# A two-layer hybrid trunk on one core: the convolution's layer norm, q's projection and the gates in another order

## The chip, the core and the metric

The kernel runs on one core of a Trainium2 chip. The metric is the device time of one launch in microseconds (us); lower is better. The core has five engines that each run their own queue of instructions in order: PE (matrix multiply, with PEld for its weight loads), DVE (vector), ACT (scalar functions and copies), POOL (a second vector engine) and SP, whose queue here starts nearly all the transfers (DMA). An engine that waits for a semaphore holds up all that is queued behind on the same engine.

## What is computed

Two layers over 512 latent tokens and 256 context tokens of width 1024. In each layer a normalised and modulated input feeds three branches, which are gated, added and projected; a gated feed-forward part (FFN) with a short convolution follows. The second layer computes the queries, gates and FFN for the 512 latents only. Cut to what matters:

```
h = modulate(rms_norm(x, g1), sh1, sc1)          # sh, sc, g from silu(c) @ w_mod + b_mod  ("mod")
z_glu, z_qa, z_kva, z_kr, z_gq, z_gk, z_gv, z_gate = split(h @ w_in)
# branch 1: convolution of 31 taps along the tokens, 512 channels
y  = a * sigmoid(g)                               # a, g = split(z_glu)
br_conv = silu(layer_norm(depthwise_conv(y) + b)) @ w_conv_out
# branch 2: MLA, 8 heads;  q from z_qa, k and v from z_kva and z_kr
q_m = rope(rms_norm(rms_norm(z_qa) @ w_q_b));  k_m = rope(rms_norm([k_nope, z_kr]))
# branch 3: GQA, 8 heads on 2 kv heads
q_g = rope(rms_norm(z_gq));  k_g = rope(rms_norm(z_gk))
merged = gate0 * br_conv + gate1 * (softmax(q_m k_m) v_m @ w_mla_o) + gate2 * (softmax(q_g k_g) v_g @ w_gqa_o)
x = x + g1 * merged @ w_out                       # gate = sigmoid(z_gate + b_gate)
x = x + g2 * conv_ffn(modulate(rms_norm(x, g2n), sh2, sc2))
```

## The kernel before

**Products.** A float32 product is made of three matmuls on halves: each operand is split into a rounded part (hi) and the rest (lo), and hi·hi, lo·hi and hi·lo are added in PSUM (`gemm`, L220 in the rows). For a weight block ACT makes hi by a copy (L138) and DVE makes lo by a subtraction (L144).

**The feeder.** Weight blocks of 128x1024 (512 KB) come in by DMA from SP's queue (L191) in the order in which the steps need them. There are 4 raw buffers and 4 pairs of split buffers. A block that is split leaves its raw buffer as soon as hi and lo are made. The blocks of a "mod" step (the adaLN weights, two blocks for each step) are not split: PE multiplies with them as they are (L383), and their two raw buffers come free only when that has run. A next load is asked for when a step has ended.

**Steps and background work.** The program is a list of steps. Before a step's function runs, `pump(budget)` takes closures from a queue `bgq`, whose items carry a cost, until the budget is used up; an item `None` ends the pumping at once. So the order in which the instructions of DVE, ACT and PE stand is fixed when the program is built: a budget decides how many background items stand between two steps. The background work of a layer is, in this order: the taps of the depthwise convolution (one DVE instruction each, L147, name acc), q's norm and rotation (`q_post`), that of GQA's q and k (`g_post`), the layer norm (LN) of the convolution (`ln_start`), and then k's norm (`k_post`), pushed when the attention begins.

**The steps of a layer.** The convolution's input (glu), three blocks of q's latent and two of kv's (`latent`, name z), 12 gate blocks (`gate`, name gt), then the token projections (`tok`: kkv in 3 steps, gq in 4, name tk), q's projection `qproj` (name qp) from three w_qb blocks, 12 more gates, `kvproj`, the attention, the merge of the branches, the out-projection and the FFN. While there are mods left, `bg_step` puts one mod step behind a gate (the first 22 in layer 0) or behind a pair of FFN up blocks j (18 in layer 0's FFN); in layer 1 none are left.

**The layer norm.** `ln_start` pushes: a (sum of the four channel blocks, three DVE instructions, name la), b (two or one matmuls of that sum with ones, name mu), c (deviation and squares), d (column sums by PE, name cs, and rstd on DVE), e (broadcast by PE, name bc, to the tile lrb), and for each channel block g: multiply by rstd on DVE (acc), sigmoid on ACT (L816, name lsg), multiply on DVE, split for the output projection. `ln_check`, called by each gate, starts it at the first gate at which `bgq` is empty. That is gate 22 in layer 0, so that d, e and g are pumped out by the slots of the attention, and gate 20 in layer 1.

**The attention.** 8 groups of two heads; a group has 14 slots in layer 0 and 12 in layer 1. A slot puts out the scores of one key block (L1126, name st), its exponential on ACT (L1133, name pe), the product with v (L1148, name ox), the row maxima of the next heads (matmul L974 on PE, reduction L976 on DVE, name mx, their transposition L995, name mt). In the first three groups each slot also pumps 0.3 of background work; what is left is put out before group 3. `norm1` of a group (L1165, name dx) stands at slot 4 of the next one, so dx marks where a group ends.

Of the kernel before, what the change touches and what calls it, by code (L numbers as in the profile page):

```python
# [96 lines left out]
def trunk_kernel(ctx: ExitStack, tc: tile.TileContext, x_t, ctx_t, cc, vec, grow, ident, rope,  # L97
# [361 lines left out]
    def layer(l):  # L459
# [7 lines left out]
        bud, gbud = (3.3, 4.2) if last else (5.0, 6.5)  # L467
# [145 lines left out]
        for i in range(2):  # L613
            latent(i, "kva", aseg, V_GKVA, 11 + i)

# [73 lines left out]
        def qproj(b):  # L689
# [14 lines left out]
            st.pop("qa")  # L704
            q_post()

        def q_post():
# [33 lines left out]
            g_post()  # L741

        def g_post():
            for (c0, nh, g0, ts_) in ((512, 2, G_GK, 6), (0, 8, G_GQ, nq)):
# [29 lines left out]
                bgq.extend((0.38 * nh, c(t)) for t in range(ts_))  # L774

        def ln_start(_):
# [30 lines left out]
            def g(j):  # L807
                def fn():
                    a_, sg = acc[j], [half("lsg") for _ in qseg]
                    b_ = a_  # L810
                    hi, lo = big("ch", F32R), big("cl", F32R)
                    for s, t in zip(qseg, sg):
                        c0, n, _ = s
                        stt(b_[:, c0:c0 + n], a_[:, cseg(s)], vcol(V_LG + j), z["rb"][:, c0:c0 + n],
                            ALU.mult, ALU.mult)
                        act(out=t[:, 0:n], in_=b_[:, c0:c0 + n], func=AF.Sigmoid, bias=vcol(V_LB + j))  # L816
                        stt(b_[:, c0:c0 + n], b_[:, c0:c0 + n], vcol(V_LB + j), t[:, 0:n], ALU.add, ALU.mult)
                    cpA(hi[:, :nT], b_[:, :nT])
                    tt(P, lo[:, :nT], b_[:, :nT], f(hi[:, :nT]), ALU.subtract)
                    z["o", j] = hi, lo  # L820
# [15 lines left out]
            for j in range(4):  # L836
                if j > 1:
                    bgq.append((0, spill(j - 2)))
                bgq.append((2.0, g(j)))
            bgq.extend([None, (0, spill(2)), None, (0, spill(3))])  # L840
# [6 lines left out]
        def ln_check():  # L847
            if not (bgq or st.get("ln")):
                st["ln"] = True
                ln_start(None)  # L850

        def gate(i):
            br, m = i % 3, i // 3

            def fn(b):
                gate_spill()
                pz = [(psum("gt"), s) for s in qseg]
# [5 lines left out]
                ln_check()  # L863
            add([W(w_gate[l, br * KD + m], 1024)], fn, gbud)
        for i in range(24):
            if i == 12:
                tok(lambda bi, n: w_kkv[l, :, bi * 864:bi * 864 + n], 3, 3, 288, 6, kkv_evac,
                    tb=(4.0, 4.0, 1.0))
                tok(lambda bi, n: w_gq[l, bi], 4, 2, 512, nq, gq_evac, lat_rstd,
                    (2.5, 0.3, 2.5, 1.5) if last else (4.0, 0.5, 4.5, 2.5))  # L870
                add([W(w_qb[l, k], 768) for k in range(3)], qproj, 4.0 if last else 6.0)
            gate(i)
            if i < 22:
                bg_step()

        def attn_pre(_):
            st.pop("H"), st.pop("ln")
# [763 lines left out]
```

## Time and profile before

| | |
|---|---|
| median of 3 runs | 2532.14 us (2530.42 to 2533.91) |
| the profiled execution, its time | 2531.37 us |
| its span, first to last instruction | 2529.6 us |
| PE busy | 2403.5 us (95% of the span) |
| DVE busy | 1464.1 us (58%) |
| ACT busy | 917.8 us (36%) |
| POOL busy | 431.6 us (17%) |
| mean granted clock of PE | 0.971 |

A busy share is an average over stages. Where the share of PE falls, the rows show who it waits for. A line of the timeline gives start, duration, engine, line of the code, and in brackets the idle time ahead of the instruction with what ended it. The granted clock is 1.00 at 2.4 GHz and 0.5 at 1.2 GHz.

### The profile page before, as it was taken

The page shows a single profiled execution, that of the slowest core. Times are in us where ns is not written, and L with a number is a line of the kernel's source. Part 1 is how long each engine was busy: PE and PEld are TensorE (multiplying, and loading weights), DVE is VectorE, ACT ScalarE, POOL GpSimd, SP SyncE. Part 2 cuts the span into 40 slices and gives each one's busy share as a digit, 9 for nine tenths or more (in the row PEclk, how much of TensorE's full clock was granted, in tenths as well). Part 3 has the DMA queues.
Part 4 walks back from the last instruction along what each step waited for, and adds up shares of the span by engine and source line. Part 5 has one row for each costly group of instructions (what it writes and reads, how often), then busy time and mean ns, then how long its engine had stood idle before and what let it go on. Part 6 is the DMA issues. An engine that isn't in the chain of part 4 may idle for free.

```text
span 2529.6 us, 32127 instructions
## 1 busy us (share of the span) xinstructions
PE 2403.5 (95%) x12434; PEld 1885.4 (75%) x12434; DVE 1464.1 (58%) x2522; ACT 917.8 (36%) x1517; POOL 431.6 (17%) x327
## 2 busy tenths in 40 slices
PE   6999999969999999999999999999769999999999
PEld 4887887634568878888888877888534578888887
DVE  5688466666524455444344457887676455655454
ACT  4322232566632234223132333324465523434332
POOL 1000000145544121001000011000046631201000
PEclk9999999979999999999999999999879999999999
DMA  6236336311044413323222233343311154232332
GB/s 254 77 113 210 123 106 206 95 57 58 26 167 142 147 37 100 101 91 118 92 101 92 82 104 102 102 121 103 91 51 39 60 183 139 80 111 78 100 102 72
DMA packets 108740, 267.56 MB, mean 106 GB/s; under 512 B 19574, under 2 KB 28412, under 8 KB 108588
## 3 DMA queue, kind: packets, MB, share of 16 engines
q1 hardware_dynamic: 108588, 265.52, 32.3%
q8 instruction: 98, 1.61, 0.3%
q14 instruction: 54, 0.44, 0.1%
HBM read 231.24 MB, written 31.60 MB: 104 GB/s over the span
## 4 chain that ended last, share of the span: by engine, by line
PE 67%; DVE 8%; ACT 3%; issue 2%; DMA 0%; POOL 0%; SPq 0%; ACTq 0%; POOLq 0%; DVEq 0%
PE up L220 22%; PE pz L220 16%; PE bx L220 7%; PE gt L220 4%; PE st L1126 4%; PE ox L1148 3%; PE tk L634 2%; DVE mx L976 2%; PE mx L974 1%; PE z L220 1%; PE tp L964 1%; PE mod L383 1%; DVE rst L144 1%; PE dx L1165 1%; PE st L1131 1%
## 5 line engine op out<-in xcount | busy, mean ns | idle before, releaser
L144 DVE TENSOR_TENSOR lo<-raw,hi 128x1024 fp32r<-128x1024 f32 (+3 forms) x282 | 345.7, 1232 | 457.7 <-ACT hi L138 451.4
L138 ACT ACTIVATE hi<-raw 128x1024 fp32r<-128x1024 f32 (+4 forms) x298 | 283.5, 963 | 467.9 <-PE pz L220 172.2
L220 PE MATMUL up<-hl,hi 128*128 128x512 f32 (+1 forms) x1088 | 330.8, 352 | 6.5 <-DVE hl L147 5.8
L220 PE MATMUL up<-hh,hi 128*128 128x512 f32 (+1 forms) x1088 | 332.4, 353 | 2.6 <-DVE fc L147 2.6
L220 PE MATMUL up<-hh,lo 128*128 128x512 f32 (+1 forms) x1088 | 330.0, 351 | 0.8 <-DVE lo L144 0.8
L147 DVE SCALAR_TENSOR_TENSOR fc<-up,vct,fc 128x511 f32<-128x511 f32 (+1 forms) x264 | 162.1, 655 | 186.3 <-ACT fc L1460 184.4
L220 PEld LDWEIGHTS up<-hh,hi 128*128 128x128 f32 x1088 | 182.8, 188 | 44.1 <-ACT fc L1460 11.7
L147 DVE SCALAR_TENSOR_TENSOR acc<-y,vct,acc 128x768 f32<-128x768 f32 (+29 forms) x240 | 211.6, 884 | 6.7
L220 PEld LDWEIGHTS up<-hl,hi 128*128 128x128 f32 x1088 | 182.8, 188 | 36.9 <-DVE hl L147 6.6
L220 PEld LDWEIGHTS up<-hh,lo 128*128 128x128 f32 x1088 | 183.0, 188 | 31.0 <-DVE lo L144 1.2
L144 POOL TENSOR_TENSOR gl<-fc,gh 128x768 fp32r<-128x768 f32 (+1 forms) x44 | 69.5, 1579 | 787.0 <-ACT gh L138 767.2
L976 DVE TENSOR_REDUCE mx<-mx 128x1 f32<-128x512 f32 (+1 forms) x288 | 140.4, 533 | 71.3 <-PE mx L974 70.4
L144 POOL TENSOR_TENSOR es<-es,pe 128x512 f32<-128x512 f32 x128 | 164.4, 1292 | 94.7 <-ACT pe L1133 91.5
L220 PE MATMUL gt<-hh,hi 128*128 128x512 f32 x576 | 177.1, 361 | 0.0
L220 PE MATMUL gt<-hh,lo 128*128 128x512 f32 x576 | 174.1, 356 | 1.5 <-DVE lo L144 1.5
L220 PE MATMUL gt<-hl,hi 128*128 128x512 f32 x576 | 174.0, 356 | 0.0
L144 POOL TENSOR_TENSOR es<-pe,pe 128x512 f32<-128x512 f32 x32 | 40.9, 1287 | 770.1 <-DMA raw<-in_w_br_dram 732.6
L220 PE MATMUL pz<-gh,hi 128*128 128x512 f32 (+1 forms) x528 | 163.6, 358 | 0.0
L220 PE MATMUL pz<-gh,lo 128*128 128x512 f32 (+1 forms) x528 | 163.2, 357 | 0.0
L220 PE MATMUL pz<-gl,hi 128*128 128x512 f32 (+1 forms) x528 | 162.7, 356 | 0.0
L1460 ACT ACTIVATE fc<-up,vct 128x512 f32<-128x512 f32 (+1 forms) x132 | 88.3, 703 | 200.6 <-PE up L220 200.6
L1133 ACT ACTIVATE pe<-st 128x512 f32<-128x512 f32 x208 | 122.7, 597 | 87.6 <-PE st L1126 72.0
(282 smaller groups left out, 4362.4 us busy)
## 6 DMA issues: line engine op xcount, KB each, us to landing
raw<-in_w_up_dram SPq DMA_DIRECT2D x88, 512.0 KB
raw<-in_w_mod_dram SPq DMA_DIRECT2D x80, 512.0 KB
raw<-in_w_gate_dram SPq DMA_DIRECT2D x48, 512.0 KB
raw<-in_w_a_dram SPq DMA_DIRECT2D x26, 512.0 KB
gd<-go SPq DMA_DIRECT2D x48, 256.0 KB
gx<-gd SPq DMA_DIRECT2D x48, 256.0 KB
raw<-in_w_dn_dram SPq DMA_DIRECT2D x32, 384.0 KB
raw<-in_w_dn_dram SPq DMA_DIRECT2D x32, 320.0 KB
```

Of the source, the lines that this page charges most:

```text
L138: act(out=o, in_=i, func=AF.Copy, scale=scale)
L144: e.tensor_tensor(out=o, in0=a, in1=b, op=op)
L147: V.scalar_tensor_tensor(out=o, in0=a, scalar=s, in1=b, op0=op0, op1=op1)
L220: mm(p[:, 0:cn], lhsT=w, rhs=a[:, c0:c0 + cn], start=(k == 0 and j == 0), stop=(k == n - 1 and j == 2))
L383: mm(p[32 * j:32 * j + 32, :], lhsT=cs[:, 2 * kt:2 * kt + 32], rhs=b[j // 2][:, (j % 2) * 512:(j % 2 + 1) * 512], start=(kt == 0), stop=(k ...
L634: mm(p[:, 0:ncols], lhsT=a, rhs=ww, start=(k == 0 and q == 0), stop=(k == KD - 1 and q == 2))
L964: nc.tensor.transpose(p[0:rows, i * 128:(i + 1) * 128], src(t0 + i), idn[:])
L976: V.tensor_reduce(out=self.m2[:, o:o + 1], in_=p[:, 0:n], axis=AX.X, op=ALU.max)
L1126: mm(p[:], lhsT=a, rhs=b, start=(k == 0), stop=(k == len(ops) - 1))
L1133: act(out=e[:], in_=p[:], func=AF.Exp, scale=hd.scale)
L1148: mm(self.o[g][64 * j:64 * j + 64, :], lhsT=self.heads[h].v(t), rhs=self.e.pop((h, i))[:], start=(t == 0), stop=(t == 5), tile_position=(0 ...
L1460: act(out=acc[:, c], in_=p[:, 0:s[1]], func=AF.Identity, scale=vcol(o + 1), bias=vcol(V_FB + j + i * KF))
```

## The change

`qproj` and its three weight blocks stand right behind the latents, in front of the gates. `qproj` starts the layer norm itself: the items of LN and of `q_post` are interleaved, and each `None` of LN (a pause before a step that needs a result of another engine) is replaced by about 3.0 of cost of `q_post` items. The items g of LN are split in two (g up to the sigmoid, g2 behind it). `g_post` is queued by a step without blocks behind the gq projection, and its last item sets a mark that `attn_pre` pumps for, so the attention begins with none of this work left. 16 gates, each with a mod in layer 0, stand ahead of the token projections instead of 12, and no mod stands behind the other 8. The six mods that layer 0's gates lose are taken up by its FFN: four of the up pairs (j = 4, 8, 12, 16) are followed by two mods instead of one, and two pairs that had none get one. Some budgets change; `lat_rstd` moves from the second gq step to gate 1.

```
-        bud, gbud = (3.3, 4.2) if last else (5.0, 6.5)
+        bud, gbud = (3.3, 4.4) if last else (5.0, 6.5)
...
             latent(i, "kva", aseg, V_GKVA, 11 + i)
+        add([W(w_qb[l, k], 768) for k in range(3)], lambda b: qproj(b), 4.0 if last else 6.0)
...
             st.pop("qa")
+            k = len(bgq)
             q_post()
+            q = [bgq.pop() for _ in range(len(bgq) - k)]
+            ln_start(None)
+            ln = [bgq.pop() for _ in range(len(bgq) - k)]
+            while ln:
+                x, n = ln.pop(), 3.0
+                while q and x is None and n > 0:
+                    n -= q[-1][0]
+                    bgq.append(q.pop())
+                if x is not None or n == 3.0:
+                    bgq.append(x)
+            bgq.extend(reversed(q))
...
             bgq.extend((2.8, c(t)) for t in range(nq))
-            g_post()
...
                 bgq.extend((0.38 * nh, c(t)) for t in range(ts_))
+            bgq.append((0, lambda: st.update(gd=l)))
...
+                    a_, z["sg", j] = acc[j], [half("lsg") for _ in qseg]
+                    for s, t in zip(qseg, z["sg", j]):
+                        c0, n, _ = s
+                        stt(a_[:, c0:c0 + n], a_[:, cseg(s)], vcol(V_LG + j), z["rb"][:, c0:c0 + n],
+                            ALU.mult, ALU.mult)
+                        act(out=t[:, 0:n], in_=a_[:, c0:c0 + n], func=AF.Sigmoid, bias=vcol(V_LB + j))
+                return fn
+
+            def g2(j):
+                def fn():
+                    a_ = acc[j]
                     hi, lo = big("ch", F32R), big("cl", F32R)
...
+                    for (c0, n, _), t in zip(qseg, z.pop(("sg", j))):
+                        stt(a_[:, c0:c0 + n], a_[:, c0:c0 + n], vcol(V_LB + j), t[:, 0:n], ALU.add, ALU.mult)
+                    cpA(hi[:, :nT], a_[:, :nT])
+                    tt(P, lo[:, :nT], a_[:, :nT], f(hi[:, :nT]), ALU.subtract)
...
-            for j in range(4):
+            for j in range(5):
+                if j < 4:
+                    bgq.append((1.1, g(j)))
+                if j > 0:
+                    bgq.append((1.1, g2(j - 1)))
                 if j > 1:
                     bgq.append((0, spill(j - 2)))
-                bgq.append((2.0, g(j)))
-            bgq.extend([None, (0, spill(2)), None, (0, spill(3))])
+            bgq.extend([None, (0, spill(3))])
...
-        def ln_check():
-            if not (bgq or st.get("ln")):
-                st["ln"] = True
-                ln_start(None)
-
...
                 gate_spill()
+                if i == 1:
+                    lat_rstd()
...
         for i in range(24):
-            if i == 12:
+            if i == 16:
...
-                tok(lambda bi, n: w_gq[l, bi], 4, 2, 512, nq, gq_evac, lat_rstd,
-                    (2.5, 0.3, 2.5, 1.5) if last else (4.0, 0.5, 4.5, 2.5))
-                add([W(w_qb[l, k], 768) for k in range(3)], qproj, 4.0 if last else 6.0)
+                tok(lambda bi, n: w_gq[l, bi], 4, 2, 512, nq, gq_evac, None,
+                    (2.5, 2.5, 2.5, 1.5) if last else (4.5, 4.5, 4.5, 2.5))
+                add([], lambda b: g_post())
             gate(i)
-            if i < 22:
+            if i < 16:
                 bg_step()
...
             gate_spill()
+            while st.get("gd") != l:
+                pump(1e9)
...
-                bg_step()
+                bg_step(2 if j in (4, 8, 12, 16) else 1)
```

Three places of the order. First ACT's queue in layer 0 where the attention begins, before; pe are the exponentials, lsg the sigmoids of LN, ch its split, and a table load stands between the two functions.

```order
L1133 ACTIVATE pe_4498<-st_4495 128x512
L138 ACTIVATE lrb_4515<-bc_4516 128x512
L138 ACTIVATE lrb_4515<-bc_4522 128x256
L816 ACT_TABLE_LOAD
L816 ACTIVATE lsg_4526<-acc_787,vct 128x512
L816 ACTIVATE lsg_4527<-acc_787,vct 128x256
L138 ACTIVATE ch_4528<-acc_787 128x768
L1133 ACT_TABLE_LOAD
L1133 ACTIVATE pe_4541<-st_4538 128x512
L816 ACT_TABLE_LOAD
L816 ACTIVATE lsg_4562<-acc_856,vct 128x512
```

And after, the place where the same sigmoids stand now, behind gate 15 in the first token projection (mrow is the copy of a mod's result, hi that of a weight block):

```order
L138 ACTIVATE lrb_3063<-bc_3064 128x512
L138 ACTIVATE lrb_3063<-bc_3070 128x256
L827 ACTIVATE lsg_3074<-acc_787,vct 128x512
L827 ACTIVATE lsg_3075<-acc_787,vct 128x256
L827 ACTIVATE lsg_3080<-acc_856,vct 128x512
L827 ACTIVATE lsg_3081<-acc_856,vct 128x256
L138 ACTIVATE ch_3086<-acc_787 128x768
L827 ACTIVATE lsg_3092<-acc_981,vct 128x512
L827 ACTIVATE lsg_3093<-acc_981,vct 128x256
L138 ACTIVATE hi_3160<-raw_2981 128x1024
```

The sigmoids of LN now stand among copies, with no exponential near them and no table load between, and in the whole program 16 table loads are gone from ACT.

Second, DVE's queue in layer 1 around a of LN, before; gt is GQA's q under `g_post`, lo are weight blocks.

```order
L144 TENSOR_TENSOR gt_14141<-gt_14141,rt_14967 128x512
L144 TENSOR_TENSOR lo_15003<-raw_14749,hi_15002 128x1024
L144 TENSOR_TENSOR la_15008<-acc_13072,acc_13240 128x512
L144 TENSOR_TENSOR lb_15009<-acc_13078,acc_13162 128x512
L144 TENSOR_TENSOR la_15008<-la_15008,lb_15009 128x512
```

And after:

```order
L147 SCALAR_TENSOR_TENSOR acc_13234<-y_13233,vct,acc_13234 128x498
L147 SCALAR_TENSOR_TENSOR acc_13234<-y_13233,vct,acc_13234 128x497
L144 TENSOR_TENSOR la_14195<-acc_13065,acc_13234 128x512
L144 TENSOR_TENSOR lb_14196<-acc_13071,acc_13156 128x512
L144 TENSOR_TENSOR la_14195<-la_14195,lb_14196 128x512
L688 TENSOR_REDUCE qss_14200<-hs_14201 128x8
```

a of LN now follows the last tap at gate 13, instead of all of `g_post`; the matmul mu that reads la stands at gate 15 on PE.

Third, SP's queue in layer 0's FFN around j = 4, before; a mod step takes two of the rows in_w_mod.

```order
L191 DMA raw_8702<-in_w_up_dram 128x1024
L191 DMA raw_8708<-in_w_up_dram 128x1024
L191 DMA raw_8714<-in_w_mod_dram 128x1024
L191 DMA raw_8716<-in_w_mod_dram 128x1024
L191 DMA raw_8844<-in_w_up_dram 128x1024
L191 DMA raw_8850<-in_w_up_dram 128x1024
```

And after:

```order
L191 DMA raw_8654<-in_w_up_dram 128x1024
L191 DMA raw_8660<-in_w_up_dram 128x1024
L191 DMA raw_8666<-in_w_mod_dram 128x1024
L191 DMA raw_8668<-in_w_mod_dram 128x1024
L191 DMA raw_8794<-in_w_mod_dram 128x1024
L191 DMA raw_8796<-in_w_mod_dram 128x1024
L191 DMA raw_8922<-in_w_up_dram 128x1024
L191 DMA raw_8928<-in_w_up_dram 128x1024
```

At this place four mod blocks in a row stand ahead of the next up block, where there were two.

## Rows read from the trace of the kernel before

**Rows 1.** The page: busy time (share, instructions) and PE's clock by slices.

```profile
PE 2403.5 (95%) x12434; PEld 1885.4 (75%) x12434; DVE 1464.1 (58%) x2522; ACT 917.8 (36%) x1517; POOL 431.6 (17%) x327
...
PEclk9999999979999999999999999999879999999999
```

**Rows 2.** The waits of PE: in all, times, longest.

```profile
PE mt L995 <- DVE mxs L144: 30.1, 16, 6.8
...
PE mu L790 <- DVE la L144: 12.8, 1, 12.8
PE st L1126 <- DVE mx L976: 9.7, 4, 4.1
PE mx L974 <- DVE mx L976: 9.1, 6, 4.8
```

**Rows 3.** Busy time by stretch; columns as in the first line.

```profile
core 0: us, PE busy (x) PEld busy (x) DVE busy (x) ACT busy (x) POOL busy (x), PEclk, DMA share, GB/s
481.12:545.35 64.23, 43.73 (x162) 24.89 (x160) 36.63 (x77) 44.65 (x80) 23.84 (x17) 0.68 0.20 71
545.35:578.62 33.27, 28.53 (x113) 13.89 (x113) 26.51 (x55) 15.62 (x36) 18.82 (x22) 0.85 0.17 49
578.62:606.57 27.95, 24.99 (x125) 13.30 (x125) 18.69 (x39) 17.34 (x40) 16.74 (x14) 1.00 0.17 51
...
1826.91:1877.99 51.08, 33.77 (x120) 17.41 (x118) 33.47 (x54) 36.10 (x60) 19.57 (x16) 0.70 0.19 65
1877.99:1906.32 28.33, 22.68 (x79) 10.32 (x79) 20.70 (x48) 13.18 (x29) 17.36 (x21) 0.82 0.14 38
1906.32:1928.02 21.70, 19.94 (x92) 9.95 (x91) 15.45 (x31) 13.10 (x30) 18.22 (x16) 1.00 0.14 44
```

**Rows 4.** Groups of ACT by form: table loads for LN's sigmoid (8) and back.

```profile
L816 ACT ACT_TABLE_LOAD x8 | 10.3, 1283 | 4.2 <-DVE acc L147 2.0 <-issue 2.0
L1133 ACT ACT_TABLE_LOAD x8 | 10.3, 1283 | 0.1
```

**Rows 5.** Timeline, layer 0's attention: LN's column sums on PE, a wait of PE.

```profile
485.41 1.77 PE L253 MATMUL cs<-ones,ssq 128*128 128x1 f32 x12 [0.48 <-ACT pe L1133]
...
503.02 0.50 PE L1126 MATMUL st<-qs,kk 128*128 128x512 f32 x1 [3.90 <-DVE mx L976]
```

**Rows 6.** Timeline of layer 1, DVE and one PE row, latents to LN.

```profile
1549.84 3.83 DVE L147 SCALAR_TENSOR_TENSOR acc<-y,vct,acc 128x497 f32<-128x497 f32 x5
...
1604.45 1.23 DVE L144 TENSOR_TENSOR lo<-raw,hi 128x1024 fp32r<-128x1024 f32 x1 [1.49 <-ACT hi L138]
...
1612.37 4.67 DVE L147 SCALAR_TENSOR_TENSOR acc<-y,vct,acc 128x507 f32<-128x507 f32 x6
...
1699.32 0.96 DVE L144 TENSOR_TENSOR lo<-raw,hi 128x768 fp32r<-128x768 f32 x1 [3.89 <-ACT hi L138]
...
1712.66 0.56 DVE L141 COPY qm<-qp 128x384 f32<-128x384 f32 x1 [0.17 <-PE qp L699]
...
1788.63 0.68 DVE L144 TENSOR_TENSOR la<-acc,acc 128x512 f32<-128x512 f32 x1
...
1790.70 2.08 PE L790 MATMUL mu<-la,ones 128*128 128x512 f32 x2 [12.82 <-DVE la L144]
```

**Rows 7.** The chain that ended last: layer 1's first 12 gates, q's projection.

```profile
1597.55 66.79 PE gt L220 x288
...
1709.65 12.57 PE qp L699 x72
```

**Rows 8.** Timeline, layer 0's FFN around one mod step.

```profile
1012.32 1.07 PE L383 MATMUL mod<-raw,cs 128*32 128x512 f32 x8
1013.42 0.80 SPq L191 DMA_DIRECT2D raw<-in_w_up_dram  x2
1017.15 1.99 ACT L138 ACTIVATE hi<-raw 128x1024 fp32r<-128x1024 f32 x2
1018.24 2.12 DVE L144 TENSOR_TENSOR lo<-raw,hi 128x1024 fp32r<-128x1024 f32 x1 [1.93 <-ACT hi L138]
```

**Rows 9.** Busy time and clock of three stretches, columns as in rows 3.

```profile
905.00:909.00 4.00, 2.05 (x18) 1.84 (x16) 3.69 (x12) 0.24 (x1) 2.38 (x1) 1.00 0.10 20
909.00:912.00 3.00, 2.86 (x15) 2.86 (x16) 1.55 (x4) 1.02 (x2) 0.00 (x0) 0.62 0.40 153
...
509.00:537.00 28.00, 14.66 (x36) 6.47 (x37) 11.24 (x21) 20.66 (x35) 12.61 (x8) 0.52 0.22 85
```

More of the change, by code (lines that the diff above doesn't have):

```diff
@@ L808, in fn @@
                 def fn():
-                    a_, sg = acc[j], [half("lsg") for _ in qseg]
-                    b_ = a_
-                    hi, lo = big("ch", F32R), big("cl", F32R)
[L812 to L819, printed above, removed]
+                    a_, z["sg", j] = acc[j], [half("lsg") for _ in qseg]
[8 more added lines that the diff above has]
+                    a_ = acc[j]
+                    hi, lo = big("ch", F32R), big("cl", F32R)
+                    for (c0, n, _), t in zip(qseg, z.pop(("sg", j))):
+                        stt(a_[:, c0:c0 + n], a_[:, c0:c0 + n], vcol(V_LB + j), t[:, 0:n], ALU.add, ALU.mult)
+                    cpA(hi[:, :nT], a_[:, :nT])
+                    tt(P, lo[:, :nT], a_[:, :nT], f(hi[:, :nT]), ALU.subtract)
                     z["o", j] = hi, lo
@@ L862, in fn @@
                     st["gs"].append((gate_d[l][m][br][:, s[0]:s[0] + s[1]], o[:, 0:s[1]]))
-                ln_check()
             add([W(w_gate[l, br * KD + m], 1024)], fn, gbud)
         for i in range(24):
-            if i == 12:
+            if i == 16:
                 tok(lambda bi, n: w_kkv[l, :, bi * 864:bi * 864 + n], 3, 3, 288, 6, kkv_evac,
                     tb=(4.0, 4.0, 1.0))
-                tok(lambda bi, n: w_gq[l, bi], 4, 2, 512, nq, gq_evac, lat_rstd,
-                    (2.5, 0.3, 2.5, 1.5) if last else (4.0, 0.5, 4.5, 2.5))
-                add([W(w_qb[l, k], 768) for k in range(3)], qproj, 4.0 if last else 6.0)
+                tok(lambda bi, n: w_gq[l, bi], 4, 2, 512, nq, gq_evac, None,
+                    (2.5, 2.5, 2.5, 1.5) if last else (4.5, 4.5, 4.5, 2.5))
+                add([], lambda b: g_post())
             gate(i)
-            if i < 22:
+            if i < 16:
                 bg_step()
         def attn_pre(_):
-            st.pop("H"), st.pop("ln")
+            st.pop("H")
             gate_spill()
+            while st.get("gd") != l:
+                pump(1e9)
         add([], attn_pre)
```

## The prediction

> **What bounds the kernel now.** I read the busy times first [rows 1]: PE is busy for 2403.5 of 2529.6 us, so all that a new order can win is 126 us of idle time, and the time in which PE runs at half rate. The clock by slices shows where that is: it falls below 9 at slices 9, 29 and 30. The waits of PE [rows 2] name what it waits for: maxima of the attention (mt, st and mx behind DVE, 30.1 + 9.7 + 9.1 = 48.9 us) and one wait of 12.8 us at LN's matmul mu in layer 1. Then I cut the attention by the marks dx [rows 3]. A later group takes 27.95 us in layer 0 (14 slots, clock 1.00) and 21.70 us in layer 1 (12 slots, clock 1.00). The first stretch, which holds 18 slots in layer 0 (one group and four slots of the next) and 16 in layer 1, takes 64.23 and 51.08 us with the clock at 0.68 and 0.70, and the second 33.27 and 28.33 us. ACT is busy for 44.65 us of the first stretch, more than DVE: LN's sigmoids are put out between the exponentials, and 16 table loads of 1283 ns lie around them [rows 4]. A reduction of a maximum queued on DVE behind LN's multiplications then comes late, and PE waits, for 3.90 us at one place [rows 5].
>
> **The attention, layer 0.** The change empties the background queue before the attention, so LN's d, e and g are gone from the first stretch, and k's norm begins at its first slot. 18 slots at the later pace are 18 x 27.95 / 14 = 35.9 us. For k's norm I take what the second stretch, which holds most of it, costs over a later one: 33.27 - 27.95 = 5.3 us. That makes 41.2 instead of 64.2: -23.0. The second stretch gives back its own 5.3, since k's norm is through by then. What PE did for LN there doesn't vanish: the column sums cs took 1.77 us [rows 5], the broadcast bc I estimate at as much, and both now run among the gates: +3.6. Layer 0: **-24.7**. For k's norm the bounds are 0 (hidden) and about 10 (twice the row, as it now meets the start of the pipeline).
>
> **Layer 1.** The same way: 16 x 21.70 / 12 = 28.9, and 28.33 - 21.70 = 6.6 for k's norm, 35.5 instead of 51.1: -15.6; second stretch -6.6; cs and bc for four columns instead of six, 3.6 x 4 / 6: +2.4. Layer 1: **-19.8**.
>
> **Mu in layer 1.** Mu waited because a of LN stood behind all of GQA's norm. It now stands behind the last tap, and the 12.8 us go. But the new place isn't free. DVE ran 14.8 us behind PE at the first gate: gate 0 begins at 1597.55 [rows 7], and the taps pumped ahead of it at 1612.37 [rows 6]. Five taps (3.83 us at 1549.84) now stand later, since the pause item that ends a pump in the FFN's tail lies elsewhere. The q projection stands between latents and gates: PE needs 12.57 us for it, DVE only three lo of 0.96, four copies of 0.56 and six taps, 2.9 + 2.2 + 4.7 = 9.8. So DVE is about 14.8 - 3.8 - 2.8 = 8.2 us behind at the new first gate. A gate costs PE 66.79 / 12 = 5.57 us and DVE one lo (1.23) and six taps (4.67), 5.9: over 13 gates it falls behind by another 4.3, to 12.5. LN's a takes 3 x 0.68 = 2.0 and stands ahead of gate 13's matmuls, mu ahead of gate 15's, two gates or 11.1 us on: mu waits 12.5 + 2.0 - 11.1 = 3.4 us. The third w_qb block finds its split buffer taken until the last latent is done: I estimate 1.1 us, one copy, about as long as a lo [rows 6]. Together -12.8 + 4.5 = **-8.3**; the new waits are bounded by 0 and 12.8, the wait that was there. In layer 0 six taps stand ahead of a PSUM copy that the projection's last tiles need: **+0.8**, what is left of the 4.67 us beyond the next tile's 3.1 (12.57 / 4) and one copy; bounds 0 and 4.7.
>
> **Mods.** Six mods leave layer 0's gates for its FFN. As PE work (1.07 us each) that is nothing. But at j = 4, 8, 12 and 16 two mods follow each other, whose four blocks hold all four raw buffers, so the next weight block is asked for only when the first mod is done. The same chain with one mod is in the trace [rows 8]: the mod ends at 1012.32 + 1.07 = 1013.39, SP starts the load at 1013.42, the first of two copies ends at 1017.15 + 1.0 = 1018.15. Today another block is there and PE goes on. With two mods PE finishes the second at 1014.46 and waits 3.7 us for hi; the third product needs lo, which ends at 1018.24 + 2.12 = 1020.36, 2.2 later, of which the first two products of 768 columns cover 0.7 (1.5 x 66.79 / 288 = 0.35 each, [rows 7]): 1.5 more. 5.2 a site, four sites: **+20.8**. Lower bound: 4 x 4.3 = 17 with a lo of 1.23 us; upper 4 x 7.5 = 30 if each wait grew to twice its hi part; and 0 if the buffers were free in time, which is a rival. Behind such a gap the clock may fall. At 905 to 909 PE was idle for half of 4 us, and the clock of the next 3 us was 0.62 [rows 9], which loses 0.38 x 3 = 1.1 us: four sites, 0 to 4.6, I take **+2**.
>
> **Sum.** -24.7 - 19.8 - 8.3 + 0.8 + 20.8 + 2 = -29.2, so 2531.4 - 29.2 = 2502.2 for the profiled execution. The median of before lies 0.8 us above it; I forecast 2502.5.
>
> **Rivals.** *(a) The FFN's buffers are free in time.* Then the 22.8 us of the doubled mods are not paid: 2479.7. For it: SP is mostly idle and ACT's copy needs only 1 us. Against: SP's order puts four mod blocks in a row, and four raw buffers are all there are.
> *(b) DVE doesn't catch up in layer 1.* LN's items now precede GQA's norm, so all of DVE's work must fit under 24 gates. If it ends behind PE, splits and the first maxima wait; the trace allows up to 12.8 us once more where I took 4.5, so about 8 to 9 on top: 2511. For it: 5.9 against 5.57 a gate. Against: the eight last gates have mostly GQA's norm beside them.
> *(c) Only ACT's table loads come back.* If LN's other work was hidden, the attention gives back 16 x 1.283 = 20.5 us [rows 4] instead of 44.5: 2526.5. For it: ACT is the busiest engine after PE there. Against: 48.9 us of PE's waits name DVE. The Trainium skill (ScalarE: Activation LUTs, What ACT_TABLE_LOAD costs) puts a switch at about 2.7 us, load and drain together; the rows show 1283 ns for the load and no gap of such size behind it. By that rule the 16 loads would be worth some 43 us, and this case would come out at about 2504, close to the forecast by another way.
> *(d) K's norm takes LN's place.* It now begins at the very slots in which LN was put out, on DVE, ACT and POOL. If it costs all that LN did, the attention gives back nothing: 2502.5 + 44.5 = 2547, slower; from a return below some 10 us on the whole is slower than before by over 5 us. For it: the second stretch, with k's norm, has DVE busy for 26.51 of 33.27 us. Against: that stretch is only 5.3 us longer than a free one, at clock 0.85 [rows 3].
> *(e) The clock stays down behind the doubled mods.* The longest stretch at half rate in the trace is 28 us at 0.52 [rows 9], which loses 13.4 us; four times 53.8 instead of 2: 2554. It decides from about 9 us lost a site. For it: PE's gap of 5 us is longer than the 2 us of idle time ahead of the fall at 909 us. Against: in that stretch PE worked 14.66 of 28 us, since it waited again and again, while behind the FFN's gap its work is dense. The Trainium skill (TensorE: Matmul & The Clock Gate, HAM oscillation) says that a matmul kernel that waits for DMA again and again swings between the two rates and loses much; it speaks against this change, and 2554 is what it would make of it. Here the rows at 909 us show a short fall, so (e) gets a small chance.
> That the LN stays in the attention isn't possible, since the order shows it ahead.
>
> **Numbers.** Forecast 0.60, (a) 0.12, (b) 0.13, (c) 0.06, (d) 0.04, (e) 0.05. The range from 2481 to 2518 holds the forecast with the bounds of k's norm and the doubled mods, (b), and half of (a); (c), (d), (e) and the other half of (a), 2 in 10, stay out. 0.2% (5 us) is about what a measurement of this kernel can tell from no change. Faster: forecast, (a), (b) and part of (c), 0.87; within: the rest of (c) and part of (d), 0.05; slower: 0.08.
>
> **What would show it.** Right: ACT has 16 table loads less; the first stretches take 41 and 35 us and the second 28 and 22, at clock near 1.00; mu in layer 1 waits for 3 us; and four new waits of PE for hi and lo of some 5 us in layer 0's FFN, each with a short fall of the clock. Wrong: first stretches still above 50 us, or no new wait in the FFN, or stretches of 10 us and more at half rate behind it, or gates of layer 1 that wait for lo one after the other.

## The result, and the profile after

The changed kernel takes 2489.2 us (median of 4 runs, 2487.56 to 2490.25) against 2531.5 us before (2530.42 to 2533.91): a ratio of 0.9836, 95% interval 0.9824 to 0.9847. That is 42 us faster; the forecast was 29, with a range of 2481 to 2518 that holds the time. The profiled execution has a span of 2488.4 us, 41.2 less than before.

The page of the kernel after, first two parts (busy time; clock by slices), to be read beside [rows 1]:

```profile
PE 2383.3 (96%) x12434; PEld 1881.3 (76%) x12434; DVE 1450.9 (58%) x2522; ACT 895.8 (36%) x1501; POOL 431.8 (17%) x327
...
PEclk9999999999999999999999999999989999999999
```

The number of matmuls is the same; ACT has 16 instructions less. PE's busy time fell by 20 us although its work is the same, since less of it runs at half rate; one slice instead of three is below 9. The waits of PE after (in all, times, longest), beside [rows 2]:

```profile
PE up L220 <- ACT hi L138: 13.1, 3, 4.6
PE mt L1014 <- DVE mxs L144: 11.9, 15, 1.7
PE mt L1014 <- DVE rst L144: 9.1, 2, 4.9
...
PE mx L993 <- DVE qs L144: 6.0, 3, 2.8
PE tp L983 <- DVE gt L144: 5.8, 2, 3.7
```

The 30.1 us of mt behind DVE became 11.9 + 9.1 (rst is a step of k's norm), and mu's 12.8 us are gone. New are the waits for hi in the FFN, as forecast, and a wait of the attention's first transposition (tp) for GQA's q, which was not. The wait of mx for the split of q (qs), 0.9 us before, is 6.0 now. The attention after, stretch by stretch (columns as in [rows 3]), first layer 0, then layer 1:

```profile
474.26:516.49 42.23, 32.67 (x137) 18.78 (x136) 31.63 (x71) 25.32 (x58) 19.35 (x21) 0.84 0.12 33
516.49:541.72 25.23, 22.98 (x113) 12.03 (x113) 17.52 (x34) 15.21 (x35) 17.26 (x16) 1.00 0.22 64
541.72:568.84 27.12, 24.57 (x125) 13.19 (x124) 17.45 (x37) 17.55 (x42) 14.54 (x11) 1.00 0.18 53
...
1808.16:1844.01 35.85, 27.41 (x105) 14.37 (x103) 26.95 (x57) 21.31 (x46) 18.23 (x20) 0.81 0.12 34
1844.01:1864.51 20.50, 18.22 (x79) 8.79 (x78) 13.84 (x28) 11.45 (x26) 17.99 (x17) 1.00 0.20 53
1864.51:1885.56 21.05, 19.69 (x91) 10.02 (x91) 13.32 (x27) 13.00 (x30) 14.28 (x12) 1.00 0.18 45
```

The first stretches went from 64.23 to 42.23 and from 51.08 to 35.85 us. ACT, busy for 44.65 us of the first before, has 25.32 us left there. Cut at PE's first matmul of a kind, the whole span divides as follows (us; the forecast by the terms of the prediction, with the six mods' 6.4 us of PE work put where they run):

| stage | before | after | change | forecast |
|---|---|---|---|---|
| start to the end of the latents | 151.0 | 150.8 | -0.3 | 0 |
| layer 0, gates, tokens, q | 307.4 | 302.0 | -5.5 | -2.0 |
| layer 0, kv projection and attention | 276.7 | 241.8 | -34.9 | -28.3 |
| layer 0, merge, out-projection | 182.2 | 177.2 | -5.0 | 0 |
| layer 0, FFN | 592.5 | 625.9 | +33.4 | +29.2 |
| layer 1 up to the attention | 295.4 | 287.6 | -7.9 | -5.9 |
| layer 1, kv projection and attention | 222.3 | 200.0 | -22.3 | -22.2 |
| the rest | 502.0 | 503.2 | +1.2 | 0 |
| sum | 2529.6 | 2488.4 | -41.2 | -29.2 |

So 76 us are gained, nearly all in the attentions and around them. Layer 0's FFN takes 33 us more, 6.4 of them the work of the six mods that the gates no longer have, and the rest of the program 1 us more.

### The profile page after: what moved, and what is told of

Same layout as the page of the kernel before. It is cut to its first block, busy times and chain, and to the rows that moved or that the text cites. A ratio compares the mean times of both kernels' runs of the same rounds, so it can differ in the third digit from the quotient of the medians.

```text
span 2488.4 us, 32116 instructions
## 1 busy us (share of the span) xinstructions
PE 2383.3 (96%) x12434; PEld 1881.3 (76%) x12434; DVE 1450.9 (58%) x2522; ACT 895.8 (36%) x1501; POOL 431.8 (17%) x327
## 4 chain that ended last, share of the span: by engine, by line
PE 86%; DVE 9%; ACT 3%; issue 1%; DMA 1%; SPq 0%; POOL 0%; ACTq 0%; DVEq 0%; POOLq 0%
PE up L220 24%; PE pz L220 16%; PE gt L220 11%; PE bx L220 7%; PE tk L635 4%; PE st L1145 4%; PE ox L1167 3%; PE z L220 3%; DVE mx L995 2%; PE gl L220 2%; PE mx L993 2%; PE mod L383 1%; PE qp L700 1%; PE ga L220 1%; PE gg L220 1%
## 5 line engine op out<-in xcount | busy, mean ns | idle before, releaser
L144 DVE TENSOR_TENSOR lo<-raw,hi 128x1024 fp32r<-128x1024 f32 (+5 forms) x282 | 342.9, 1222 | 451.4 <-ACT hi L138 441.5
L138 ACT ACTIVATE hi<-raw 128x1024 fp32r<-128x1024 f32 (+3 forms) x298 | 284.0, 963 | 421.0 <-PE pz L220 176.6
L220 PE MATMUL up<-hh,lo 128*128 128x512 f32 (+1 forms) x1088 | 335.1, 356 | 1.2 <-DVE lo L144 1.2
L220 PEld LDWEIGHTS gt<-hh,hi 128*128 128x128 f32 x576 | 95.6, 189 | 26.5 <-ACT go L879 9.2
```

The lines of the kernel that those rows point to most:

```text
L138: act(out=o, in_=i, func=AF.Copy, scale=scale)
L144: e.tensor_tensor(out=o, in0=a, in1=b, op=op)
L220: mm(p[:, 0:cn], lhsT=w, rhs=a[:, c0:c0 + cn], start=(k == 0 and j == 0), stop=(k == n - 1 and j == 2))
```

## Experiment 1: one mod at a time, as before

```
-            if i < 16:
+            if i < 22:
                 bg_step()
...
-                bg_step(2 if j in (4, 8, 12, 16) else 1)
+                bg_step()
```

> The changed kernel with one part undone: a mod behind each of the first 22 gates and one mod behind each FFN pair, so no two mods follow each other. Theory (the changed kernel pays 16.9 us of waits for hi, about 9 us of half clock behind them and 6.4 us of mods in layer 0's FFN, and 6.4 us less in its gates): 27 us faster than the changed kernel, about 2462, with no wait of PE for hi in the FFN and the granted clock at 1.00 there. Rival (six mods behind the last gates of layer 0 hold raw buffers where the background work is short, so that the gates wait instead): the FFN loses 33 us, but the gates win back more than the 6.4, and the time stays above 2475.

Measured: 2473.5 us, 15.7 us faster than the changed kernel; ratio to the kernel before 0.9779 (0.9764 to 0.9793). The FFN gives back 30.2 us and none of its waits is left, as the theory says. But only half of it arrives. The gates take 7.2 us more, 6.4 of which are the six mods. And the attention of layer 0, in which no instruction differs, takes 247.0 instead of 241.8 us: its later groups are again at 27.84, 28.46, 29.19 and 29.18 us, as long as before the change [rows 3 show 27.95 for the first of these]. So something about where the mods stand slows the attention; experiment 5 takes that up.

## Experiment 2: the doubled mods alone, in the kernel before

```
-            if i < 22:
+            if i < 16:
                 bg_step()
...
-                bg_step()
+                bg_step(2 if j in (4, 8, 12, 16) else 1)
```

> The kernel before with only this part of the change: mods behind the first 16 gates and two mods behind FFN pairs 4, 8, 12 and 16. Theory (the price lies in the raw buffers alone and does not need the rest of the change): slower than before by 27 us, about 2558, with four waits of PE for hi of 4 to 4.6 us in layer 0's FFN and a stretch at half rate behind each. Rival (the price comes from the rest of the change, for instance from another phase of DVE and ACT at the FFN's start): slower by under 10 us.

Measured: 2547.0 us against 2530.2 for the kernel before, 16.8 us slower; ratio 1.0066 (1.0051 to 1.0081). The FFN of layer 0 goes from 592.5 to 621.6 us, and PE's four waits for hi are there with 4.65, 4.48, 3.84 and 4.00 us. The price thus needs nothing of the rest of the change, as the theory says. The gates take 7.4 us less, 6.4 of which are the six mods that the theory had counted. The miss of 10 us has two larger sources: the attention of layer 0, whose LN is untouched here, takes 5.9 us less, and the FFN loses 29.2 us where the changed kernel loses 33.4. The waits are the same there, but behind the first two of them the clock falls for a shorter time (granted 0.78 and 0.78 over the next 7.9 us, against 0.67 and 0.72 in the changed kernel).

## Experiment 3: the table loads put back

```
                     if hs:
                         self.score(2 * g + s % 2, s // 2)
+                    if g == 0 and s in (3, 5, 7, 9):
+                        warm(AF.Sigmoid)
```

> The changed kernel with four one-column sigmoids in slots 3, 5, 7 and 9 of the first group of each layer's attention, which bring back the 16 table loads of 1283 ns (20.5 us of ACT) and nothing else of the layer norm. Theory (the layer norm cost the attention mainly by waits of PE for DVE, whose results stood behind ACT's sigmoids): at most 8 us slower than the changed kernel, up to 2497. Rival (the table loads are what the attention paid): 20 us slower, about 2510; with the Trainium skill's price of a switch (ScalarE: Activation LUTs) 43 us, about 2532.

Measured: 2495.9 us, 6.7 us slower than the changed kernel. The loads, by form of ACT's instructions (count, busy time, mean ns):

```profile
L153 ACT ACT_TABLE_LOAD x13 | 16.7, 1283 | 0.2
L1152 ACT ACT_TABLE_LOAD x8 | 10.3, 1283 | 0.1
```

Of the 13, 5 are in the changed kernel too. So 16 switches, 20.5 us of ACT, cost the program 6.7 us; by the trace 5.0 of it lie in the two attentions. ACT is idle for 0.2 and 0.1 us in all ahead of the loads of these two rows. By the Trainium skill (ScalarE: Activation LUTs, What ACT_TABLE_LOAD costs) the 16 switches would cost some 43 us, an estimate at about 2.7 us each, load and drain together; the trace doesn't agree. Rival (c) falls, by the table above too, since the two attentions gave back 57 us and not 20.5.

In this run nothing waits for the sigmoids, though. In the kernel before, DVE's multiplications wait for them, with two loads ahead of the sigmoid, and a maximum stands behind the multiplications:

```profile
512.67 1.28 ACT L1133 ACT_TABLE_LOAD   x1
...
514.58 1.28 ACT L816 ACT_TABLE_LOAD   x1
515.87 0.72 ACT L816 ACTIVATE lsg<-acc,vct 128x512 f32<-128x512 f32 x1
516.63 0.75 DVE L147 SCALAR_TENSOR_TENSOR acc<-acc,vct,lsg 128x512 f32<-128x512 f32 x1 [3.26 <-ACT lsg L816]
...
518.81 1.01 DVE L976 TENSOR_REDUCE mx<-mx 128x1 f32<-128x512 f32 x2
519.55 1.01 PE L974 MATMUL mx<-kk,qs 128*128 128x512 f32 x2 [1.81 <-DVE mx L976]
```

So what LN cost the attention went over DVE: multiplications that waited for ACT, and maxima that waited behind them. How much of that the loads inside this chain made is open, since no run has LN in the attention without its loads.

## Experiment 4: the attention without k's norm

The branch's k is only scaled by a constant and its rotated part is zero, so the time is that of a kernel that computes something else. It leaves out 25 items of background work.

```
-            bgq.extend((0.6, a(t)) for t in range(6))
-            bgq.extend([(0.6, b), (0.8, b1)] + rsqrt_parts(z, 48) + [(0.2, b2)])
-            for t in range(6):
-                bgq.extend(c(t))
+            for t in range(6):
+                kv = K[t][:, :T].rearrange("p (h e) -> p h e", h=8)
+                P.memset(kv[:, :, NOPE:QK], 0.0)
```

> The changed kernel without k's norm and rotation in the MLA branch (k is scaled by a constant in the copy that is there anyway, its rotated part set to zero by six POOL instructions, which the time should be read with). Theory (k's norm is what the first stretch of the attention costs over its steady pace, 6.3 us in layer 0 and 7 in layer 1): both first stretches go to about 36 and 29 us, and the kernel is some 13 us faster than the changed one, about 2476. Rival (the first stretch is long because the pipeline fills): under 4 us faster.

Measured: 2472.5 us, 16.7 us faster. The first stretch of layer 0 falls from 42.2 to 32.0 us, by 10.3 (its first mt at 471.61, the dx at 503.56); that of layer 1 from 35.85 to 28.96, by 6.9. So k's norm is what the first stretch costs over its own pace. But that pace is 32.0 us in layer 0, not the 35.9 which the prediction took from a later group, and the norm costs 10.3, not 5.3. The prediction's first stretch of layer 0 came out right, 41.2 against 42.2, by two errors of opposite sign, which is luck. In layer 1 both parts hold: 28.9 and 6.6 were forecast.

## Experiment 5: a bank of PSUM held through the attention

A mod's sum runs over eight steps, and it keeps its PSUM bank from the first to the last. With a mod behind 22 gates the sum of a third group is begun at gate 16 and is finished only in the FFN. With 16 mods, two groups of eight, no sum is open in between.

```
         def attn_pre(_):
             st.pop("H")
+            if not last:
+                st["hold"] = psum("hold")
+                mm(st["hold"][:, 0:128], lhsT=ones[:], rhs=ones[:], start=True, stop=True)
...
+                    if not last:
+                        cpA(small("hd")[:, 0:1], st.pop("hold")[:, 0:1])
```

> The changed kernel with one PSUM bank of eight held from the attention of layer 0 to its FFN (written once by a small matmul, read by a one-column copy at the end). In the kernel before, and with a mod behind 22 gates, the sum of the mods of layer 1's first part is begun at gate 16 and stays open until the FFN, so one bank is taken through the attention; with 16 mods none is open. Theory (this bank is what shortens the later groups by 0.7 us each, the second stretch by some 2, and nothing else differs): the groups of layer 0 go back to 27.8, 28.5, 29.2, 29.2 us, the attention of layer 0 loses 5 us, and the kernel takes about 2494. Rival (the later groups are shorter since LN's rows have left, and the bank means nothing): within 2 us of the changed kernel.

Measured: 2497.1 us, 7.9 us slower than the changed kernel. Busy time by stretch, layer 0's attention with the bank held (columns as in [rows 3]):

```profile
542.55:570.39 27.84, 24.98 (x124) 13.31 (x124) 17.50 (x36) 17.33 (x40) 14.59 (x11) 1.00 0.17 51
570.39:598.86 28.47, 25.94 (x131) 14.17 (x130) 16.58 (x34) 17.02 (x40) 14.64 (x11) 1.00 0.13 43
598.86:628.04 29.18, 27.69 (x140) 16.19 (x141) 15.58 (x35) 17.62 (x40) 14.62 (x11) 1.00 0.13 42
```

And the same stretches of the changed kernel, the second and third of them:

```profile
568.84:596.62 27.78, 25.55 (x131) 14.17 (x130) 16.37 (x34) 16.93 (x40) 14.59 (x11) 1.00 0.13 44
596.62:625.11 28.49, 27.46 (x140) 16.11 (x141) 15.32 (x35) 17.62 (x40) 14.59 (x11) 1.00 0.13 43
```

At a clock of 1.00 in both, each group is 0.7 us longer with seven banks than with eight, to within 0.1 us the length before the change. The kv projection and attention take 246.6 instead of 241.8 us. The trace shows what waits. With the bank held, a row maximum (mx) waits for the copy qh out of PSUM,

```profile
580.73 0.39 PE L996 MATMUL mx<-kh,qh 96*128 96x256 f32 x1 [0.42 <-ACT qh L138]
```

while at the same place of the changed kernel both mx run before that copy has ended, and only the mt behind them waits for it:

```profile
578.23 0.51 PE L993 MATMUL mx<-kh,qh 96*128 96x512 f32 x2
579.12 0.30 PE L1014 MATMUL mt<-idn,mxs 128*64 128x128 f32 x1 [0.38 <-ACT qh L138]
```

So mx doesn't need what the copy writes, but the bank that it frees; here it starts 0.7 us later in its group. 5 us of the gain in layer 0's attention thus come from the bank and not from LN. The rest of this run's 7.9 us lies in stages in which it differs by nothing (by the trace 1.7 us in the merge and 0.8 in layer 1 up to the attention) and is within what such stages vary between runs: the merge took 177.2, 178.9, 180.3 and 182.1 us in the changed kernel and in experiments 1, 3 and 4, with the same instructions on PE.

## Experiment 6: the same mods, no two in a row

```
                 one(0)
+                if j in (4, 8, 12, 16):
+                    bg_step()
                 one(1)
-                bg_step(2 if j in (4, 8, 12, 16) else 1)
+                bg_step()
```

> The changed kernel with the second mod of pairs 4, 8, 12 and 16 put between the two up blocks of the pair instead of behind the first mod, so that the same 24 mods run in the FFN and no two follow each other. Theory (the price of the doubled mods is the raw buffers that two mods in a row hold, and the half clock behind the wait): no wait for hi in layer 0's FFN, clock 1.00 there, some 24 us faster than the changed kernel, about 2465. Rival (24 mods in this FFN are more than the raw buffers carry, wherever they stand): waits of 2 us and more behind each of the eight mods of these pairs, over 2480.

Measured: 2462.1 us (2458.71 to 2464.64), 27 us faster than the changed kernel; ratio to the kernel before 0.9731 (0.9713 to 0.9749). It is the fastest kernel of this study. First the changed kernel at j = 4, timeline: two mods, the loads that SP starts when the first has run, the first hi and lo, and PE's next matmul.

```profile
965.54 1.92 PE L383 MATMUL mod<-raw,cs 128*32 128x512 f32 x16
966.63 1.66 SPq L191 DMA_DIRECT2D raw<-in_w_up_dram  x2
...
970.99 1.06 ACT L138 ACTIVATE hi<-raw 128x1024 fp32r<-128x1024 f32 x1 [0.53 <-DMA raw<-in_w_up_dram]
972.08 1.42 DVE L144 TENSOR_TENSOR lo<-raw,hi 128x1024 fp32r<-128x1024 f32 x1 [2.56 <-ACT hi L138]
972.10 1.01 PE L220 MATMUL up<-hh,hi 128*128 128x512 f32 x2 [4.63 <-ACT hi L138]
```

Its busy time by stretch there: the wait, and then 8 us with the granted clock in the column before the last two.

```profile
967.40:972.10 4.70, 0.07 (x4) 0.00 (x1) 2.11 (x5) 1.90 (x2) 1.50 (x1) 0.82 0.83 269
972.10:976.00 3.90, 3.90 (x11) 3.17 (x12) 2.62 (x2) 1.06 (x1) 0.31 (x1) 0.50 0.84 306
976.00:980.00 4.00, 4.00 (x21) 3.48 (x20) 1.07 (x1) 1.39 (x2) 0.00 (x0) 0.84 0.56 172
```

And the same place, 14 us long, with the mods apart:

```profile
962.00:976.00 14.00, 14.00 (x83) 11.36 (x82) 7.65 (x9) 5.73 (x8) 1.87 (x1) 1.00 0.54 176
```

PE doesn't pause and the clock stays at 2.4 GHz. The FFN takes 599.1 us, the 592.5 of before and the six mods (6.4). So the doubled mods cost 625.9 - 599.1 = 26.8 us: 4.63 + 4.48 + 3.84 + 3.99 + 0.8 = 17.7 us of waits for hi and lo, and 9 us of half clock behind them. The half clock is some 2.6 us at the first site (0.50 x 3.9 + 0.16 x 4); over the 7.9 us behind each of the four waits the granted clock is 0.67, 0.72, 0.57 and 0.68.

## Experiment 7: lo on POOL in layer 1

```
-            add([W(w_gate[l, br * KD + m], 1024)], fn, gbud)
+            add([(WP if last and i % 3 == 1 else W)(w_gate[l, br * KD + m], 1024)], fn, gbud)
```

> e6_mods_apart, and in layer 1 the lo of 8 of the 24 gate blocks is made by POOL, which is idle there, instead of DVE (8 times 1.23 us). Theory (from the latents to the attention of layer 1 DVE has more to do than PE, and the waits for GQA's q at the attention's start, 2.1 and 3.7 us, are what is over): these waits go, 5 to 6 us faster than e6_mods_apart, about 2459. Rival (POOL takes 2.4 us for a lo and disturbs DVE beside it, so gates wait for lo): no faster than e6_mods_apart.

Measured: 2470.0 us, 8 us slower than experiment 6. A group of six taps on DVE beside POOL's lo, and the same six in experiment 6:

```profile
1594.45 6.77 DVE L147 SCALAR_TENSOR_TENSOR acc<-y,vct,acc 128x504 f32<-128x504 f32 x6
...
1597.50 2.40 POOL L144 TENSOR_TENSOR lo<-raw,hi 128x1024 fp32r<-128x1024 f32 x1 [16.29 <-ACT hi L138]
```

```profile
1590.87 4.62 DVE L147 SCALAR_TENSOR_TENSOR acc<-y,vct,acc 128x504 f32<-128x504 f32 x6
```

A lo on POOL (2.4 to 2.9 us) takes 1.22 us off DVE and makes the taps beside it 2.15 us longer, so DVE is later, and mu waits for 6.4 us instead of 1.65. The Trainium skill (SBUF — State Buffer, Who interferes with whom) says that a DVE instruction with two inputs from SBUF contends with a POOL instruction that reads SBUF; a tap has two, y and acc, and the rows agree.

## Experiments 8 and 9: LN queued whole, ahead of or behind q's norm

```
-            k = len(bgq)
-            q_post()
...
-            bgq.extend(reversed(q))
+            ln_start(None)
+            q_post()
```

Experiment 9 has the two calls in the other order.

> The changed kernel with LN queued whole ahead of q's norm, with its six pauses, instead of woven into it. Theory (a pause ends a pump, so up to six steps of a layer put out less than their budget, and DVE's work runs out later; in layer 1, where DVE is late anyway, each pause costs up to 4.4): 5 to 15 us slower than the changed kernel, 2494 to 2504, with longer waits at the start of layer 1's attention and none new in layer 0. Rival (the gates have room for the pauses): within 3 us.

> The changed kernel with q's norm queued ahead of LN instead of LN ahead of and woven into it; LN's six pauses stand in the queue as in e8_not_woven (2516.1). Theory (the loss of e8_not_woven comes from the pauses, which end pumps early, not from which of the two norms is first): about as slow as e8_not_woven, 2510 to 2520, with DVE's backlog waited for at the start of both attentions. Rival (LN must come first since its chain over PE and ACT is the longer one): slower than e8_not_woven by over 5 us.

Measured: 2516.1 us with LN ahead and 2504.9 with q's norm ahead, 27 and 16 us slower than the changed kernel. Neither number was foreseen: 27 is beyond the 5 to 15 of the theory, and 2504.9 is below the 2510 to 2520 of experiment 9. In experiment 8 layer 0 up to the attention takes 310.3 instead of 302.0 us and layer 1 305.7 instead of 287.6; the waits of tp for gt at layer 1's attention are 10.8, 3.53, 4.66 and 3.53 us. In experiment 9 layer 0 takes 302.2, as in the changed kernel, and layer 1 303.6, with waits of 8.99 and three times 3.53. So the direction holds: the pauses push DVE's work to the end, and in layer 1 the weaving is worth 16 us against the better of the two. But the order matters as well, against the theory of experiment 9.

DVE's order in layer 1 shows where the time goes. GQA's norm begins with the reductions gss, here of the changed kernel and of experiments 8 and 9:

```profile
1748.73 1.24 DVE L688 TENSOR_REDUCE gss<-hs 128x2 f32<-128x128 f32 x6
```

```profile
1775.07 1.25 DVE L688 TENSOR_REDUCE gss<-hs 128x2 f32<-128x128 f32 x6
```

```profile
1767.38 1.25 DVE L688 TENSOR_REDUCE gss<-hs 128x2 f32<-128x128 f32 x6
```

Counted from the layer's first matmul, that is 251.1, 269.3 and 268.2 us, and each time the kv projection starts 35 to 37 us later. In experiment 8 LN's last multiplication runs at 241.1 us, earlier than in the changed kernel (246.7), but all of q's norm (245.3 to 268) stands behind LN and its pauses; in experiment 9 q's norm is done first, and LN with its pauses ends at 259.3. Why experiment 8 also loses 8 us in layer 0, where tp waits for 4.8 and 1.1 us, and experiment 9 nothing, is argued from the same order and not shown.

## Experiments 10 and 11: what tp waits for in layer 1

Experiment 10 is experiment 6 with eight copies moved from DVE to ACT in layer 1; experiment 11 is experiment 6 with 14 gates ahead of the token projections there.

```
-                    (cpA if i else cpV)(Q[t][:, i * 384:(i + 1) * 384], p[i][:, 0:384])
+                    (cpA if i or last else cpV)(Q[t][:, i * 384:(i + 1) * 384], p[i][:, 0:384])
...
-            (cpA if t % 2 else cpV)(st["gt"][t][:, 0:512], p[:])
+            (cpA if t % 2 or last else cpV)(st["gt"][t][:, 0:512], p[:])
```

```
-            if i == 16:
+            if i == (14 if last else 16):
```

> e6_mods_apart, and in layer 1 ACT makes the eight PSUM copies of q's projection, kkv and gq that DVE made (4 of 0.55, 2 of 0.68, 0.41 and 0.18: 4.1 us of DVE). Theory (in layer 1 DVE is busy without a break from the latents to the attention, and PE's 5.8 us of waits for GQA's q are DVE's backlog; POOL's lo failed since it slowed DVE's taps, and copies on ACT do not touch DVE): 3 to 4 us faster than e6_mods_apart, about 2458, the waits of tp for gt at 2 us or less. Rival (these waits belong to the chain of the last two tiles and not to the backlog): no faster than e6_mods_apart.

> e6_mods_apart with 14 instead of 16 gates ahead of the token projections in layer 1 alone. Theory (PE's waits for GQA's q at the start of layer 1's attention, 5.8 us, come from work that can't begin before gq is there and takes DVE longer than PE needs for the gates behind; two more gates behind are 11.1 us more of cover, and DVE's pauses of 4.3 and 2.3 us in the gq steps are filled with LN): the waits of tp for gt go, 4 to 6 us faster than e6_mods_apart, about 2457. Rival (the queue is put out in order, so GQA's norm waits for the end of LN, which is as late as before): no faster than e6_mods_apart.

Measured: 2464.3 and 2467.5 us against 2462.1 in experiment 6: the first is the same within the spread of its runs, the second 5 us slower. Both theories miss, and in both the rival holds. Against a backlog speaks the timeline of DVE in the changed kernel, end of the gq steps and first gates behind them: DVE has pauses,

```profile
1728.32 1.23 DVE L144 TENSOR_TENSOR lo<-raw,hi 128x1024 fp32r<-128x1024 f32 x1 [4.33 <-ACT hi L138]
...
1735.30 1.23 DVE L144 TENSOR_TENSOR lo<-raw,hi 128x1024 fp32r<-128x1024 f32 x1 [2.27 <-ACT hi L138]
...
1742.52 1.23 DVE L144 TENSOR_TENSOR lo<-raw,hi 128x1024 fp32r<-128x1024 f32 x1 [2.32 <-ACT hi L138]
```

and with the copies gone from DVE the pause at the second place grows from 2.27 to 4.42 us, while the waits of tp stay at 2.12 and 3.65. From about 1750 us on DVE has no pause until PE needs the last tile at 1785. So what counts is when GQA's norm begins, and in the queue it stands behind LN's end. Counted from the layer's first matmul (us):

| run | GQA's norm begins | layer 1 up to the attention |
|---|---|---|
| changed kernel | 251.1 | 287.6 |
| experiment 6 | 251.6 | 288.1 |
| experiment 10 | 252.6 | 289.1 |
| experiment 11 | 255.5 | 292.0 |
| experiment 1 | 250.6 | 287.5 |

With two more gates behind, DVE's pauses of 4.34, 2.36 and 2.29 us are still there, the norm begins later and not earlier, and tp waits for 1.6, 4.8 and 3.5 us. Experiment 1 adds a warning: there no tp waits in layer 1, since PE comes 6.1 us later (it waited 3.1 us for hi at q's projection, and the background work stands in another order), and the layer's part is as long as with the wait. So a wait of tp that goes isn't a gain unless GQA's norm begins earlier. Whether larger budgets in the gq steps would fill the pauses wasn't tried and stays open.

## Why the prediction was right, point by point

**The attention.** The mechanism holds in both layers, and in layer 1 the sizes too: -22.2 forecast, -22.3 measured. In layer 0 the term of the first stretch was right in sum and wrong in its parts (experiment 4): the step that failed there is the pace, taken from a later group. In layer 0 6.6 us came on top. The step that failed is the sentence on the mods that, as PE work, moving six of them is nothing: besides work a mod has a PSUM bank, and 16 mods leave none open. That is worth 5 us (experiments 1, 2 and 5). Rivals (c) and (d) fall: the attentions gave back far more than the loads' 20.5 us, which put back alone cost 6.7, and k's norm in LN's place costs 10 us in layer 0 and 7 in layer 1. The argument for (c) read its row too low: ACT's 44.65 us in the first stretch are more than PE's 43.73.

**The doubled mods.** Right in mechanism and place, four waits at j = 4, 8, 12 and 16; 26.8 us against 22.8. The waits for hi were a little longer than forecast (16.9 against 14.8), those for lo nearly absent (0.8 against 6.0), since PE, at half rate behind the wait, hardly ever reaches lo before DVE does; the clock was under-sized (9 against 2), since I took half of one short fall [rows 9] for a wait that is longer than the idle time in that row. It is far from rival (e)'s 13.4 us a site, as the rows had spoken for. That experiment 2 pays 22.8 us (29.2 less the six mods' 6.4), the forecast to the digit, is luck: its waits are those of the changed kernel, and only the clock fell for a shorter time. Rival (a) falls with experiment 2.

**Mu and layer 1.** The wait of 12.8 us went as forecast. The new one that I put at 3.4 us is 0.2, and none for the third w_qb block is there; instead tp waits for 5.8 us at the attention's start. The working summed DVE's lag gate by gate up to mu and stopped there. It should have gone on to the next place where PE needs DVE, and there the reason is another one: GQA's norm doesn't start early enough (experiments 8 to 11). Together layer 1's part came out at -7.9 against -5.9. Rival (b) is half of what happened: a wait of its kind, but of 6 us and included in a sum that was better than forecast.

**Layer 0's gates and merge.** The gates gained 5.5 us where I had 2.0. Half a microsecond of that is cs and bc, which take 1.50 and 1.60 us there instead of the 3.6 that I took from the attention, where cs ran at half rate [rows 5]. The 0.8 us of new wait isn't there, and two waits of before, 0.8 us of a cs and 1.5 us of a gate for its lo, are gone, which the forecast left out. The 5.0 us of the merge can't be put down to the change: its granted clock was 0.97 before and 1.00 after, and kernels with the changed order and the same instructions on PE there have 177 to 182 us.

Of the 12 us by which the profiled execution is better than forecast, 5 are the bank, 5 a stage that varies, and the rest small terms of both signs (3.5 in the gates and 2.0 in layer 1 for it, 4.2 in the FFN against it).

## What to carry to other kernels

A step that is "only moved" takes its buffers along: look where it holds a raw buffer, a split pair or a PSUM bank, and for how long, since here a bank that an open sum kept through the attention cost 5 us and two steps in a row that hold all raw buffers cost 27. Work that changes ACT's function between exponentials is best moved out as a whole: the two attentions gained 57 us by it (5 of them by the bank), and the loads alone, put back, cost 6.7. And a pause item in a queue of background work should be filled with other work that is independent of it: unwoven, the same instructions were 16 to 27 us slower.

## What the runs showed of the hardware

A wait of PE of 4.6 us between dense stretches was followed by 3.9 us at a granted clock of 0.50 and 4 us at 0.84. Over the 7.9 us behind the four waits of the changed kernel (3.8 to 4.6 us) the granted clock was 0.67, 0.72, 0.57 and 0.68, which adds about half of the wait to its price; behind the same four waits of experiment 2 it was 0.78, 0.78, 0.59 and 0.68, so this part of the price varies between kernels. One PSUM bank less made each group of the attention 0.7 us longer. A subtraction of 128x1024 on POOL makes six taps on DVE beside it take 6.77 instead of 4.62 us, more than the 1.22 us that the subtraction would take on DVE itself.
